# Linear-attention gates in four steps per head, and the decayed context keys formed inside the levels

## The chip, the cores and the metric

The kernel runs on one NeuronCore of one Trainium2 chip. The metric is device microseconds of one execution; lower is better. Engines are named as in the profile: PE (TensorE matmuls), PEld (its weight loads), DVE (VectorE), ACT (ScalarE), POOL (GpSimd), SP (SyncE, which issues most loads).

## The reference, cut to what matters

The reference is one layer of a hybrid backbone for 256 latent tokens with a prefix of 256 context tokens and a width of 2048. One input projection feeds a windowed attention with 16 heads and a gated linear attention (GLA) with 4 heads, key width 256 and value width 512; both are merged, and a convolutional feed-forward block follows. The change lies in the GLA part, which runs in both directions:

```python
gf = log_sigmoid(lrf @ w_gate_f + b_gate_f) / 16      # and gb, its own weights
# context, need_out False: only end states
b = jnp.cumsum(g, axis=1)
w = jnp.exp(b[:, -1:] - b)
sf = einsum("bthd,bthe->bhde", k_ctx * w, v_ctx)       # sb: the same on the flipped tokens
# latent tokens, chunk by chunk, from S = sf (or sb)
o_inter = (q * exp(b)) @ S
A[t, s] = sum_d q[t, d] k[s, d] exp(b[t, d] - b[s, d])  # s <= t
o = o_inter + A @ v
```

All arithmetic is in 32-bit floats, and the depth is 1, so the context gives nothing but keys, values and end states.

## The kernel before, in words

Every large projection splits its float32 weights into a high part (`whi`, made on ACT, L207) and a low part (`wlo`, made on DVE, L208), and PE multiplies by both. `proj_nat` and `proj_T` walk over the 2048 input rows in eight pairs of 128. For each pair they load and split a 128 x 1024 weight piece (`wsplit`), run the matmuls with the high part and then those with the low part. In `proj_nat` over latent and context tokens (four token tiles) that is 16 matmuls with 512 columns, then 8.

Small work is woven into these projections. Python generators and lists hold steps, and there are two hooks per weight pair: `tick` ahead of the split, and `midway` between the high and the low matmuls. Both call `aside`, which adds a rate to a counter and resumes the generator in `beside` each time the counter passes one. The PE instructions that a step emits are pinned behind the last matmul of the projection emitted so far (`mm_b`, `turn_b`), so they can't run earlier than their hook. The instructions of other engines have no such pin. From all of this a planner lays down the order on each engine ahead of the run: it takes instructions by readiness as it estimates it, and by their order in the program. `in_order` adds a tie that orders two instructions of one engine and costs no semaphore. A tile gets one of a fixed number of buffers of its tag and waits until one is free.

The four GLA heads run one after the other through `with_gla`, beside one projection each: head 0 beside the key projection (`kb_block`), heads 1 to 3 beside the value projection of their own head (`v_block`; the last with `by_tile`, whose last pair goes tile by tile). A block has 16 hooks. `gla_A` yields between these steps:

- *Gates.* For each direction `d` and half `dt` of the key width: one matmul into `pz`, then on ACT an absolute value (L708), a relu (L710), an exponential and a logarithm (L711, L712). DVE adds the latent half into `segs` (L713), POOL the context half into `gc` (L714). Two halves make a step, so the gates take two steps.
- *Level 0 to 7.* The latent 256 x 256 matrix `A` is built from segments of doubling length m = 1, 2, ..., 128. A level makes `q2` and, from level 1 on, `k2` (two exponentials on ACT each, L753, L754, L760, L761, and a multiplication on DVE each, L755, L762), then updates the segment sums in place with two to four DVE additions (L764 to L767), of which L767 is the last. Then it issues the `products` of the level before: eight small matmuls into `pa` and a masked copy into `at` (L738). Level 1 yields once more ahead of its products.
- *Context.* After the products of level 7, `q2` and `q3` for the context (L780, L781) and the decayed context keys: four prefix scans over `gc` into `kf` and `kg` (L787, L789), the total `tot` (L791), three exponentials (L793, L794) and two multiplications with the context keys (L795, L796). Two yields later come the matmuls of `kf` and `kg` with `q2` and `q3`, and the split of the result into `atc`.

`gla_o` multiplies `ats` and `atc` with the values into `po`. Between the levels DVE also serves a background list, `mod_latent`: products of modulation rows with a sum (L365), in turns set by `bg_rate`. Behind head 3 POOL loads the rotary table into `rope`, which takes a buffer of the tag "fc" (six buffers, shared with `gc`, `ats`, `atc`), and multiplies it with the norms (L884, L886). `q2`, `k2`, `kf`, `kg` share the four buffers of tag "fa"; the gate temporaries `ge`, `gm`, the `junk` of `gla_o` and `norms` share the four of "fb".

Of the kernel before, what the change touches and what calls it, by code (L numbers as in the profile page):

```python
# [8 lines left out]
F32 = mybir.dt.float32  # L9
F32R = mybir.dt.float32r  # L10
U8 = mybir.dt.uint8
AF = mybir.ActivationFunctionType
ALU = mybir.AluOpType
# [3 lines left out]
P = 128  # L17
D = 2048
T = 256
# [12 lines left out]
def layer_kernel(ctx, tc, A, out):  # L32
    nc = tc.nc
    V, S, G, PE = nc.vector, nc.scalar, nc.gpsimd, nc.tensor
# [7 lines left out]
    sm = pool(name="sm", bufs=4)  # L42
# [7 lines left out]
    def M(name, shape, dt=F32):  # L50
        return big.tile(shape, dt, name=name, tag="M")

    def W2(tag, name, shape, dt=F32):
        return f2.tile(shape, dt, name=name, tag=tag, bufs=F2_BUFS[tag])
# [9 lines left out]
    def in_order(*ins):  # L64

        for a, b in zip(ins, ins[1:]):
            tc.add_manual_dep(b, a.name, mybir.DependencyInfo(
                mybir.DependencyClass.NoSync, mybir.DependencyReason.DATA), reason="order")
# [25 lines left out]
    def mm_b(*a, **k):  # L94
        return pe_seq(after(PE.matmul(*a, **k)))  # L95
# [33 lines left out]
    ones = cst.tile([P, P], F32, name="ones")  # L129
# [16 lines left out]
    beside = []  # L146
# [343 lines left out]
    def affine_shift(s, t0, n):  # L490
        for kt in range(t0, t0 + n):
            xk = xr[2 * s + kt // 8][:, kt % 8, :]
            sh = shift1[:, s, kt:kt + 1]
            hi, lo = hh[s][kt // 8][:, kt % 8, :], hl[s][kt // 8][:, kt % 8, :]
            j = S.activation(hi, xk, AF.Identity, bias=sh).ins
            i = V.scalar_tensor_tensor(lo, xk, sh, hi.bitcast(F32), op0=ALU.add, op1=ALU.subtract).ins
        return i, j
# [49 lines left out]
    i, j = affine_shift(0, *groups[0])  # L547
# [31 lines left out]
    i, j = affine_shift(1, *groups[1])  # L579
# [94 lines left out]
    for d in range(2):  # L674
        mk = sel[:, 32 + d:33 + d]
        S.activation(lr[:, d, :], pl, AF.Identity, scale=mk)
        for q in (32, 96):
            r = lr[q:q + 32, d, :]
            V.scalar_tensor_tensor(r, pl[q:q + 32, :], mk[q:q + 32, :], r.bitcast(F32),
                                   op0=ALU.mult, op1=ALU.subtract)  # L680
# [11 lines left out]
    def gla_A(h, kb, qb, res):  # L692
        k_ = kb[:, (h % 2) * 2:(h % 2) * 2 + 2, 0:T]
        kc = kb[:, (h % 2) * 2:(h % 2) * 2 + 2, T:2 * T]
        q_ = qb[:, 2 * h:2 * h + 2, :]
        R = M("segs", [P, 4, 2, T])
        PF, SB, SX, PX = (R[:, i] for i in range(4))
        G.memset(R[:, 2:4], 0.0)
        gc = []
        for d in range(2):  # L700
            g_ = W2("fc", "gc", [P, 2, T])
            for dt in range(2):
                f = 2 * h + dt
                pz = bank("pz", side=True)
                mm_b(pz, wg[:, f * P:(f + 1) * P], lr[:, d, :], start=True, stop=True)
                b = nbg[:, d * 8 + f:d * 8 + f + 1]
                e = W2("fb", "ge", [P, 512])
                S.activation(e, pz, AF.Abs, scale=-1.0, bias=b)  # L708
                mn = W2("fb", "gm", [P, 512])
                S.activation(mn, pz, AF.Relu, scale=-1.0, bias=b)  # L710
                S.activation(e, e, AF.Exp, scale=-1.0)  # L711
                S.activation(e, e, AF.Ln, bias=ones[:, 0:1])  # L712
                V.tensor_tensor((PF if d == 0 else SB)[:, dt, :], mn[:, 0:T], e[:, 0:T], op=ALU.add)  # L713
                G.tensor_tensor(g_[:, dt, :], mn[:, T:2 * T], e[:, T:2 * T], op=ALU.add)  # L714
            gc.append(g_)
            yield

        at = sm.tile([P, 2, P], F32, name="at", tag="at", bufs=1)
        pa = bank("pa", (P, 2, P), side=True)
        for t in range(2):  # L720
            for dt in range(2):
                mm_b(pa[:, t, :], k_[:, dt, t * P:(t + 1) * P], q_[:, dt, t * P:(t + 1) * P],
                          start=(dt == 0), stop=(dt == 1))
        V.tensor_scalar(at, pa, 2.0, None, op0=ALU.mult)

        def halves(x, m):
            v = x.rearrange("p d (n two h) -> p (d n) two h", two=2, h=m)
            return v[:, :, 0, :], v[:, :, 1, :]

        def products(lv, q2, k2):  # L730
            pa = bank("pa", (P, 2, P), side=True)
            for t in range(2):
                tq = t if lv < 7 else 1 - t
                for dt in range(2):
                    mm_b(pa[:, t, :], k2[:, dt, t * P:(t + 1) * P],
                              q2[:, dt, tq * P:(tq + 1) * P], start=(dt == 0), stop=(dt == 1))
            if lv < 7:
                V.copy_predicated(at, lmask[:, lv:lv + 1, :].to_broadcast([P, 2, P]), pa)  # L738
            else:
                split(ats[0][:, 0], ats[0][:, 1], at)  # L740
                split(ats[1][:, 0], ats[1][:, 1], pa)

        ats = [W2("fc", "ats", [P, 2, 2, P], F32R) for _ in range(2)]
        for lv in range(8):
            m = 1 << lv
            n = T // m
            pfL, pfR = halves(PF, m)
            sbL, sbR = halves(SB, m)
            sxL, sxR = halves(SX, m)
            pxL, pxR = halves(PX, m)  # L750
            q2 = W2("fa", "q2", [P, 2, T])
            qL, qR = halves(q2, m)
            S.activation(qR, pfR, AF.Exp, scale=-1.0 / 16)  # L753
            S.activation(qL, sbL, AF.Exp, scale=-1.0 / 16)  # L754
            V.tensor_tensor(q2, q2, q_, op=ALU.mult)  # L755
            k2 = k_
            if lv:
                k2 = W2("fa", "k2", [P, 2, T])
                kL, kR = halves(k2, m)
                S.activation(kL, sxL, AF.Exp, scale=-1.0 / 16)  # L760
                S.activation(kR, pxR, AF.Exp, scale=-1.0 / 16)  # L761
                V.tensor_tensor(k2, k2, k_, op=ALU.mult)  # L762
            if lv < 7:
                V.tensor_tensor(sxL, sxL, pfR[:, :, m - 1:m].to_broadcast([P, n, m]), op=ALU.add)  # L764
                V.tensor_tensor(pxR, pxR, sbL[:, :, 0:1].to_broadcast([P, n, m]), op=ALU.add)
            V.tensor_tensor(pfR, pfR, pfL[:, :, m - 1:m].to_broadcast([P, n, m]), op=ALU.add)
            V.tensor_tensor(sbL, sbL, sbR[:, :, 0:1].to_broadcast([P, n, m]), op=ALU.add)  # L767
            if lv == 1:
                yield
            if lv:  # L770
                products(lv - 1, *prev)
            prev = q2, k2
            yield
        products(7, *prev)


        q2 = W2("fa", "q2", [P, 2, T])
        q3 = W2("fa", "q3", [P, 2, T])
        for dst, e in ((q2, PF), (q3, SB)):
            S.activation(dst, e, AF.Exp, scale=-1.0 / 16)  # L780
            V.tensor_tensor(dst, dst, q_, op=ALU.mult)  # L781
        kf = W2("fa", "kf", [P, 2, T])
        kg = W2("fa", "kg", [P, 2, T])
        tot = sm.tile([P, 2], F32, name="tot", tag="tot", bufs=2)
        one = ones[:, 0:1].to_broadcast([P, T])
        for dt in range(2):
            V.tensor_tensor_scan(kf[:, dt, :], one, gc[0][:, dt, :], 0.0, op0=ALU.mult, op1=ALU.add)  # L787
            V.memset(kg[:, dt, 0:1], 0.0)
            V.tensor_tensor_scan(kg[:, dt, 1:T], ones[:, 0:1].to_broadcast([P, T - 1]), gc[1][:, dt, 0:T - 1], 0.0,  # L789
                                 op0=ALU.mult, op1=ALU.add)  # L790
        V.tensor_scalar(tot, kf[:, :, T - 1], -1.0 / 16, None, op0=ALU.mult)  # L791
        for dt in range(2):
            S.activation(kf[:, dt, :], kf[:, dt, :], AF.Exp, scale=1.0 / 16, bias=tot[:, dt:dt + 1])  # L793
        S.activation(kg, kg, AF.Exp, scale=-1.0 / 16)  # L794
        V.tensor_tensor(kf, kf, kc, op=ALU.mult)  # L795
        V.tensor_tensor(kg, kg, kc, op=ALU.mult)  # L796
        yield
        yield
        pa = bank("pa", (P, 2, T), side=True)
        for t in range(2):  # L800
            for i, (kk, qq) in enumerate(((kf, q2), (kg, q3))):
                for dt in range(2):
                    mm_b(pa[:, t, :], kk[:, dt, t * P:(t + 1) * P], qq[:, dt, :],
                              start=(i == 0 and dt == 0), stop=(i == 1 and dt == 1))
        atc = [W2("fc", "atc", [P, 2, T], F32R) for _ in range(2)]
        split(atc[0], atc[1], pa)
        res.extend((ats, atc))
# [32 lines left out]
    qbt = M("qb", [P, 8, T])  # L840
# [2 lines left out]

    def with_gla(h, kb, block):
        res = []
        beside[:] = [gla_A(h, kb, qbt, res), 0.91, 0.0]
        v = block()
        for _ in beside[0]:
            pass
        beside.clear()  # L850
        return res, v
# [322 lines left out]
    for half, blocks in enumerate((range(0, 6), range(6, 11))):  # L1174
        n = len(blocks)
# [128 lines left out]
```

## Time and profile before

| | |
|---|---|
| median of 3 runs | 1984.97 us (1984.95 to 1985.31) |
| profiled execution | 1985.05 us |
| its span, first to last instruction | 1983.1 us |
| PE busy | 1958.6 us (99%) |
| DVE busy | 1400.0 us (71%) |
| ACT busy | 971.2 us (49%) |
| granted TensorE clock | 0.999 |
| first gate matmul of heads 0 to 3 | 213.6, 278.7, 343.2, 407.2 us |

Times in rows count from the first instruction. A row of a timeline has the start, the length, the engine, the line, the operation, what it writes and reads, and, in brackets, how long the engine stood idle before it and who ended that. A row of waits has the total, the count and the longest. Lengths of consecutive instructions of an engine overlap a little.

### The profile page before, as it was taken

To read this page: it belongs to the slowest core of one execution; us is meant where nothing else is said; L and a number is where in the kernel's file an instruction comes from. 1 tells how busy PE (TensorE), PEld (TensorE's weight loads), DVE (VectorE), ACT (ScalarE), POOL (GpSimd) and SP (SyncE) were. 2 spreads that over 40 slices of the span, in tenths; PEclk is the share of its full clock that TensorE was granted. 3 is DMA by queue.
4 is the path that set the end of the run, shared out by engine and by line. 5 is a ranking of instruction groups with operands and counts; after the bars stand their busy time and mean duration, and the time that the engine had idled before them with its cause. 6 is when DMAs were issued, how large, how long until landed. Compare 5 with 4: busy or idle time off the path is not lost.

```text
span 1983.1 us, 27131 instructions
## 1 busy us (share of the span) xinstructions
PE 1958.6 (99%) x10324; PEld 1637.9 (83%) x10324; DVE 1400.0 (71%) x2150; ACT 971.2 (49%) x1413; POOL 44.5 (2%) x61
## 2 busy tenths in 40 slices
PE   7999999999999999999999999999999999999999
PEld 5679888888887788888888888888888888888887
DVE  5765667876858888777776457889887555677754
ACT  4323555553345666444444445755555334555532
POOL 0010010112000000000000000000000000000000
PEclk9999999999999999999999999999999999999999
DMA  9965222336753456888888668688886566666563
GB/s 379 413 262 178 65 85 75 107 98 196 249 156 112 127 181 210 267 289 287 295 281 272 232 224 282 193 271 278 259 275 232 192 193 190 190 190 184 190 215 113
DMA packets 183603, 420.90 MB, mean 212 GB/s; under 512 B 12544, under 2 KB 12768, under 8 KB 178736
## 3 DMA queue, kind: packets, MB, share of 16 engines
q1 hardware_dynamic: 181856, 413.19, 63.8%
q0 software_dynamic: 1440, 5.80, 1.0%
q8 instruction: 81, 1.33, 0.3%
q14 instruction: 50, 0.41, 0.1%
q10 hardware_dynamic: 176, 0.17, 0.0%
HBM read 416.98 MB, written 2.13 MB: 211 GB/s over the span
## 4 chain that ended last, share of the span: by engine, by line
PE 68%; DVE 0%; ACT 0%; issue 0%; DVEq 0%
PE acc L83 52%; PE accs L83 12%; PE poa L95 1%; PE pS L95 1%; PE ptp L98 1%; PE pto L98 0%; PE ptx L98 0%; DVE wlo L208 0%; ACT s L973 0%; PE ptq L98 0%; DVE s L978 0%; DVE yd L1225 0%; DVE yd L1219 0%; DVE raw L365 0%; ACT whi L207 0%
## 5 line engine op out<-in xcount | busy, mean ns | idle before, releaser
L208 DVE TENSOR_TENSOR wlo<-raw,whi 128x1024 fp32r<-128x1024 f32 x568 | 694.8, 1225 | 435.0 <-ACT whi L207 394.7
L207 ACT ACTIVATE whi<-raw 128x1024 fp32r<-128x1024 f32 x568 | 601.1, 1059 | 773.3 <-PE acc L83 619.4
L83 PE MATMUL accs<-h,whi 128*128 128x512 f32 x704 | 176.3, 392 | 0.0
L83 PE MATMUL acc<-h,whi 128*128 128x512 f32 x640 | 160.4, 392 | 0.0
L83 PEld LDWEIGHTS accs<-h,whi 128*128 128x128 f32 x704 | 126.6, 189 | 22.6
L83 PE MATMUL acc<-whi,h01hi 128*128 128x512 f32 x352 | 139.9, 398 | 0.0
L83 PE MATMUL acc<-whi,h00hi 128*128 128x512 f32 x352 | 139.0, 395 | 0.0
L83 PE MATMUL acc<-whi,h00lo 128*128 128x512 f32 x352 | 138.0, 392 | 0.0
L83 PE MATMUL acc<-whi,h01lo 128*128 128x512 f32 x352 | 137.9, 392 | 0.0
L83 PE MATMUL acc<-whi,al 128*128 128x512 f32 x352 | 137.0, 389 | 0.0
L83 PE MATMUL acc<-whi,ah 128*128 128x512 f32 x352 | 137.0, 389 | 0.0
L83 PEld LDWEIGHTS acc<-h,whi 128*128 128x128 f32 x640 | 115.1, 189 | 20.6
L83 PEld LDWEIGHTS accs<-h,wlo 128*128 128x128 f32 x704 | 96.0, 190 | 6.8
L83 PE MATMUL acc<-wlo,h01hi 128*128 128x512 f32 x352 | 98.7, 396 | 0.0
L83 PE MATMUL accs<-h,wlo 128*128 128x256 f32 x704 | 98.2, 282 | 0.0
L83 PE MATMUL acc<-wlo,h00hi 128*128 128x512 f32 x352 | 97.7, 394 | 0.0
L83 PE MATMUL acc<-wlo,ah 128*128 128x512 f32 x352 | 94.3, 389 | 0.0
L83 PEld LDWEIGHTS acc<-h,wlo 128*128 128x128 f32 x640 | 87.4, 190 | 6.3
L83 PE MATMUL acc<-h,wlo 128*128 128x256 f32 x640 | 89.4, 282 | 0.0
L365 DVE CUSTOM_DVE_ANT_0 raw<-raw,csrow,pack 128x1024 f32<-128x1024 f32 x64 | 81.7, 1284 | 0.0
L83 PEld LDWEIGHTS acc<-whi,ah 128*128 128x128 f32 x352 | 66.1, 188 | 13.7
L83 PEld LDWEIGHTS acc<-whi,al 128*128 128x128 f32 x352 | 66.1, 188 | 13.6
(389 smaller groups left out, 3566.0 us busy)
## 6 DMA issues: line engine op xcount, KB each, us to landing
raw<-in_w_in SPq DMA_DIRECT2D x208, 512.0 KB, 4.4
raw<-in_w_up SPq DMA_DIRECT2D x176, 512.0 KB, 3.9
raw<-in_w_modT SPq DMA_DIRECT2D x128, 512.0 KB, 4.6
raw<-in_w_down SPq DMA_DIRECT2D x88, 512.0 KB, 3.7
mraw<-in_w_mod SPq DMA_DIRECT2D x32, 1024.0 KB, 13.3
raw<-in_w_attn_o SPq DMA_DIRECT2D x32, 512.0 KB, 4.9
raw<-in_w_gla_o SPq DMA_DIRECT2D x32, 512.0 KB, 4.7
raw<-in_w_out SPq DMA_DIRECT2D x32, 512.0 KB, 4.8
```

Of the source, the lines that this page charges most:

```text
L83: r = pe_seq(PE.matmul(*a, **k))
L95: return pe_seq(after(PE.matmul(*a, **k)))
L98: return pe_seq(after(PE.transpose(*a)))
L207: j = S.activation(hi[:, 0:n, :], raw[:, 0:n, :], AF.Copy).ins
L208: i = V.tensor_tensor(lo[:, 0:n, :], raw[:, 0:n, :], hi[:, 0:n, :].bitcast(F32), op=ALU.subtract).ins
L365: i0 = V.tensor_tensor_reduce(out=raws[i], in0=raws[i], in1=row[0], scale=1.0, scalar=d if h else bmod[:, b0:b0 + 1], op0=ALU.mult, op1=AL ...
```

## The change

- Each gate piece is a step of its own: four steps in place of two. The extra yield in level 1 is gone.
- `kf` and `kg` are taken ahead of the levels, from the buffers "fb" instead of "fa". The scans of the first half follow level 2, those of the second half level 3, the total and the exponentials level 4, the multiplications level 6. Each of their DVE instructions is tied by `in_order` behind the last segment update of its level (and behind one another).
- The rate of `beside` goes from 0.91 to 0.97.

The instructions themselves stay the same in kind, number and size.

```diff
                 G.tensor_tensor(g_[:, dt, :], mn[:, T:2 * T], e[:, T:2 * T], op=ALU.add)
+                yield
             gc.append(g_)
-            yield
+
+        kf = W2("fb", "kf", [P, 2, T])
+        kg = W2("fb", "kg", [P, 2, T])
+
+        def decays(dt, level):
+            one = ones[:, 0:1].to_broadcast([P, T])
+            i = V.tensor_tensor_scan(kf[:, dt, :], one, gc[0][:, dt, :], 0.0, op0=ALU.mult, op1=ALU.add).ins
+            V.memset(kg[:, dt, 0:1], 0.0)
+            j = V.tensor_tensor_scan(kg[:, dt, 1:T], ones[:, 0:1].to_broadcast([P, T - 1]), gc[1][:, dt, 0:T - 1],
+                                     0.0, op0=ALU.mult, op1=ALU.add).ins
+            in_order(level, i, j)
+
+        def decayed(level):
+            tot = sm.tile([P, 2], F32, name="tot", tag="tot", bufs=2)
+            in_order(level, V.tensor_scalar(tot, kf[:, :, T - 1], -1.0 / 16, None, op0=ALU.mult).ins)
+            for dt in range(2):
+                S.activation(kf[:, dt, :], kf[:, dt, :], AF.Exp, scale=1.0 / 16, bias=tot[:, dt:dt + 1])
+            S.activation(kg, kg, AF.Exp, scale=-1.0 / 16)
+
+        def decayed_keys(level):
+            in_order(level, V.tensor_tensor(kf, kf, kc, op=ALU.mult).ins)
+            in_order(level, V.tensor_tensor(kg, kg, kc, op=ALU.mult).ins)
+
+        beside_levels = {2: lambda i: decays(0, i), 3: lambda i: decays(1, i), 4: decayed, 6: decayed_keys}
...
-            V.tensor_tensor(sbL, sbL, sbR[:, :, 0:1].to_broadcast([P, n, m]), op=ALU.add)
-            if lv == 1:
-                yield
+            level = V.tensor_tensor(sbL, sbL, sbR[:, :, 0:1].to_broadcast([P, n, m]), op=ALU.add).ins
             if lv:
                 products(lv - 1, *prev)
             prev = q2, k2
+            if lv in beside_levels:
+                beside_levels[lv](level)
             yield
...
-        kf = W2("fa", "kf", [P, 2, T])
-        kg = W2("fa", "kg", [P, 2, T])
-        tot = sm.tile([P, 2], F32, name="tot", tag="tot", bufs=2)
...
-        beside[:] = [gla_A(h, kb, qbt, res), 0.91, 0.0]
+        beside[:] = [gla_A(h, kb, qbt, res), 0.97, 0.0]
```

More of the change, by code (lines that the diff above doesn't have):

```diff
@@ L781, in gla_A @@
             V.tensor_tensor(dst, dst, q_, op=ALU.mult)
-        kf = W2("fa", "kf", [P, 2, T])
-        kg = W2("fa", "kg", [P, 2, T])
-        tot = sm.tile([P, 2], F32, name="tot", tag="tot", bufs=2)
[L785 to L796, printed above, removed]
         yield
```

## The prediction

> **What bounds the kernel now.** I read the page first.
>
> ```profile
> span 1983.1 us, 27131 instructions
> PE 1958.6 (99%) x10324; PEld 1637.9 (83%) x10324; DVE 1400.0 (71%) x2150; ACT 971.2 (49%) x1413; POOL 44.5 (2%) x61
> ```
>
> PE sets the end, and the change takes no matmul away. It can therefore win only time in which PE stands still inside the linear-attention (GLA) part, and lose only by new standstills. The profiled execution took 1985.05 us, 1.95 more than its span and 0.08 more than the median of the three runs. 0.2% of that is 4.0 us, about what a measurement of this kernel can tell from no change. Next I asked the view of waits for 213 to 480 us, where the four heads lie.
>
> ```profile
> PE pa L95 <- DVE q L755: 3.3, 4, 1.1
> PE pa L95 <- DVE kf L795: 2.5, 3, 1.0
> DVE kf L787 <- PE pa L95: 3.4, 2, 2.5
> ACT kg L794 <- DVE kg L789: 5.0, 2, 2.5
> POOL rope L876 <- DVE kg L788: 33.8, 1, 33.8
> ```
>
> PE waits once per head for the `q2` of level 0 (3.3 us together) and in three heads for the decayed context keys (2.5 us). Both are in the change's reach. An idle row is measured from the modelled end of a matmul, and matmuls overlap, so I looked at both places in head 1 in the timeline (start, length, engine, ...).
>
> ```profile
> 289.72 0.39 PE L83 MATMUL acc<-whi,h10hi 128*128 128x512 f32 x1
> 289.95 0.39 PE L83 MATMUL acc<-whi,h10lo 128*128 128x512 f32 x1
> 291.54 1.07 PE L83 MATMUL acc<-wlo,h00hi 128*128 128x512 f32 x4
> 293.68 1.16 PE L95 MATMUL pa<-q,kb 128*128 128x128 f32 x8 [1.08 <-DVE q L755]
> 307.75 0.62 PE L83 MATMUL acc<-wlo,h01hi 128*128 128x512 f32 x2
> 308.23 1.13 PE L95 MATMUL pa<-q,k 128*128 128x128 f32 x8
> 309.11 0.71 PE L83 MATMUL acc<-wlo,h01hi 128*128 128x512 f32 x2
> 310.80 0.39 PE L83 MATMUL acc<-whi,h01lo 128*128 128x512 f32 x1
> 311.17 1.02 PE L95 MATMUL pa<-q,k 128*128 128x128 f32 x7
> 321.69 1.05 PE L95 MATMUL pa<-q,k 128*128 128x128 f32 x8
> 328.74 0.67 PE L95 MATMUL pa<-q,kf 128*128 128x256 f32 x2 [0.54 <-DVE kf L795]
> ```
>
> Starts lie 0.23 apart (289.72, 289.95). Four from 291.54 would free PE at 292.46; it starts at 293.68, a hole of 1.22 where the row says 1.08. So a hole is 0.14 longer than its idle, and seven holes come to 3.3 + 2.5 + 7 x 0.14 = **6.8 us**. That is all there is to win.
>
> Then who is behind these waits: busy time in four stretches, each from the last gate to the decayed keys of a head (length; PE, PEld, DVE, ACT, POOL).
>
> ```profile
> 226.80:263.80 37.00, 36.00 (x305) 35.79 (x304) 32.82 (x69) 17.41 (x39) 0.00 (x0) 1.00 0.23 71
> 292.40:328.60 36.20, 34.72 (x181) 28.46 (x180) 34.31 (x71) 18.41 (x42) 0.95 (x1) 1.00 0.32 91
> 355.60:392.60 37.00, 35.79 (x188) 29.85 (x186) 35.61 (x72) 18.93 (x41) 1.53 (x2) 1.00 0.32 96
> 419.50:459.00 39.50, 37.72 (x195) 31.27 (x195) 39.05 (x78) 19.82 (x45) 2.81 (x5) 1.00 0.47 140
> ```
>
> DVE is free for 4.2, 1.9, 1.4 and 0.5 us. In heads 1 to 3 the levels and the context chain are one DVE queue, nearly without a gap: moving work inside it shortens nothing on DVE; it changes which product finds its operand late.
>
> **The change, part by part.** Rows of head 1, one of POOL and then DVE's:
>
> ```profile
> 290.59 1.48 POOL L714 TENSOR_TENSOR gc<-gm,ge 128x256 f32<-128x256 f32 x1 [0.60 <-ACT ge L712]
> ```
>
> ```profile
> 285.29 0.42 DVE L713 TENSOR_TENSOR segs<-gm,ge 128x256 f32<-128x256 f32 x1 [1.96 <-ACT ge L712]
> 289.31 0.97 DVE L713 TENSOR_TENSOR segs<-gm,ge 128x256 f32<-128x256 f32 x1
> 290.20 1.27 DVE L365 CUSTOM_DVE_ANT_0 raw<-raw,csrow,pack 128x1024 f32<-128x1024 f32 x1
> 291.40 0.95 DVE L713 TENSOR_TENSOR segs<-gm,ge 128x256 f32<-128x256 f32 x1
> 292.95 0.68 DVE L755 TENSOR_TENSOR q<-q,qb 128x512 f32<-128x512 f32 x1
> 307.39 0.68 DVE L762 TENSOR_TENSOR k<-k,kb 128x512 f32<-128x512 f32 x1
> 319.49 0.68 DVE L755 TENSOR_TENSOR q<-q,qb 128x512 f32<-128x512 f32 x1
> 321.29 1.29 DVE L781 TENSOR_TENSOR q<-q,qb 128x512 f32<-128x512 f32 x2
> 322.85 0.69 DVE L787 TENSOR_TENSOR_SCAN kf<-ones,gc 128x256 f32<-128x256 f32 x1
> 323.47 0.68 DVE L789 TENSOR_TENSOR_SCAN kg<-ones,gc 128x255 f32<-128x255 f32 x1
> 326.70 0.16 DVE L791 TENSOR_SCALAR tot<-kf 128x2 f32<-128x2 f32 x1
> 327.90 0.69 DVE L795 TENSOR_TENSOR kf<-kf,kb 128x512 f32<-128x512 f32 x1 [0.45 <-ACT kf L793]
> ```
>
> *Hooks.* A weight pair has two hooks, one before its 16 hi matmuls and one before its 8 lo ones; 16 per block. At rate 0.91 hooks 2 to 11 and 13 to 16 each run one step, at 0.97 hooks 2 to 16. Gates go from hooks 2, 3 to 2 to 5; level 0 from 4 to 6; the products of level 0 ("p0") from 6 to 7; p1 to p5 each one hook later (p5 from 11 to 12, empty before); p6, p7 and the `kf` products stay at 13, 14 and 16. The step count rises from 14 to 15, the hooks that run one too, so nothing spills behind the block.
>
> *The p0 wait.* Up to p0 PE gets the same gate matmuls and the same `at` product, and one lo part more. Without its hole PE was at p0, four lo matmuls behind hook 6, at 292.46; hook 7 is four matmuls on, at 293.4. The operand was there at 292.95 + 0.68 = 293.63. The last two gate sums L713 took 0.97 and 0.95 instead of 0.42, the second inside POOL's sum `gc` (290.59 to 292.07). With pieces a hook apart I let only the last one be so slow at the end, which brings the operand to about 293.1. So p0 waits for nothing; at worst 0.2 per head is left. Gain 3.3 + 4 x 0.14 = 3.9.
>
> *The `kf` wait.* What leaves the end is four scans at 0.62 (322.85 to 323.47), `tot` 0.1 and two multiplications of 0.69 at most (327.90), about 0.65 in a full queue: 3.9 us per head. Then the `kf` products want only the two `q` of L781, whose end moves from 322.58 to 326.5 at most; PE is there at 328.74 - 1.22 - 0.68 = 326.8 (both holes taken out). No wait: gain 2.5 + 3 x 0.14 = 2.9. The scans' wait for a "fa" buffer (the 3.4 us row) goes too, as `kf`, `kg` sit in "fb", whose gate tiles are done by level 2; next late after it are the `q` of L781.
>
> *What is queued behind the moved work.* The ties put scans, `tot` and multiplications behind a level's last update on DVE, ahead of the next level's `q2`, `k2`; PE's p3 to p7 wait for those. p7: hook 14 without the hole is 321.69 - 1.22 = 320.5; its operand came at 319.49 + 0.68 = 320.17, and comes 3.9 later less what fills idle DVE time (about 1): 323.1, so 2.6 late. p4 takes p5's old hook: 311.17 less two matmuls 0.46, one product 0.88 (308.23 to 309.11) and 1.22 makes 308.6; its operand, 308.07 before, comes four scans later, 310.5: 1.9 late. Late against its hook is not yet a wait: the order on PE is laid down beforehand by a planner, and the rows show it pushing a product back (at 308.23 p4 stands behind two lo matmuls of a part of eight, its operand 0.16 ahead of it, no idle). It costs what the planner doesn't foresee. Bounds per head: 0, if it foresees all; 3.9, if PE stands for the whole insertion. I take one slow gate sum, 0.97 - 0.42 = 0.55, which is no longer paid at p0 and runs on down a full queue, in heads 1 to 3: 1.7. It lies nearest to p0, the one error of plan that the trace shows with its cause.
>
> *POOL and the other queues.* The rope load waits 33.8 us on POOL for head 3's scans to free a "fc" buffer. Now that happens at level 3. In head 1 level 4's operand came 308.07 - 292.40 = 15.7 behind the start of the stretch, so in head 3 the load goes out near 419.5 + 15.7 = 435 instead of 455.6, and its multiplications 4.4 later, beside the last levels instead of the block's end.
>
> ```profile
> L876 POOL DMA_DIRECT2D rope<-in_k_rope x1: 544/544/544, 455.6 to 455.6; - x1
> L886 POOL TENSOR_TENSOR att<-rope,norms x8: 317/1295/1312, 460.4 to 468.5; 128x64 f32<-128x64 f32 x8
> L884 POOL TENSOR_TENSOR att<-rope,norms x4: 451/458/1438, 460.0 to 467.8; 128x128 f32<-128x128 f32 x4
> 460.07 1.42 DVE L365 CUSTOM_DVE_ANT_0 raw<-raw,csrow,pack 128x1024 f32<-128x1024 f32 x1
> 461.42 1.33 DVE L365 CUSTOM_DVE_ANT_0 raw<-raw,csrow,pack 128x1024 f32<-128x1024 f32 x1
> ```
>
> Beside them DVE's L365 takes 1.33 to 1.42 instead of 1.27. I take the lower, 0.05 for each of 12: 0.6 on a DVE with no slack. Upper bound: DVE stands for each at its shortest, 4 x 0.451 + 8 x 0.317 = 4.3. The Trainium skill ("SBUF — State Buffer", "SBUF: two separate sides") says that a DVE operation with two SBUF inputs and a GpSimd operation that reads SBUF take a shared port pair as an exclusive lock, and the second one blocks fully. By it the term would be up to the 4.3. The trace agrees only in part, as L713 beside `gc` lost 0.55 and L365 beside rope 0.06 to 0.15.
>
> ACT gets its three decay exponentials at level 4 instead of the end; it is busy for half of the stretches, so nothing. SP's loads and their order stay.
>
> **Sum.** 6.8 - 1.7 - 0.6 = 4.5 us: 1985.05 - 4.5 = 1980.55, and 0.08 less for the median: **1980.4 us**.
>
> **The rivals.** *A, the waits come back in the levels.* For it: heads 2 and 3 have 1.4 and 0.5 us of idle DVE, so the late products stay late; the three `kf` holes have no cause in the rows, and if the scans themselves run longer than planned, their 2.9 moves with them to p4. Then 6.8 - 1.7 - 0.6 - 2.9 leaves 1.6: 1983.4. If DVE stands for all of POOL's operations, 4.3 instead of 0.6, 4.5 - 3.7 leaves 0.8: 1984.2; that is what the lock would do (Trainium skill, as above). That the planner places the decays late in spite of the ties, which only forbid earlier, leaves the `kf` wait, again 1.6: 1983.4. Against it: p1 to p5 have no waits, so the planner's times for levels are good. Chance 0.30, all within 0.2%.
>
> *B, slower.* PE stands at p4 to p7 for the whole inserted work: the planner believes the operands are there and leaves the products at their hooks, while DVE is behind by 3.9 in heads 1 to 3. 11.7 - 6.8 = +4.9: 1989.9. It decides from 6.8 us of waits for `q2`, `k2` on (10.8 for 0.2%). For it: a full DVE, p7 2.6 late. Against it: the product at 308.23, placed in time. Chance 0.25.
>
> **How the numbers follow.** The forecast, faster by over 0.2% (below 1981.0), has 0.45; its own range runs from 1977.5 (all 6.8 won, and 0.7 by gates that end sooner) to 1981. A has 0.30, B 0.25. The range 1977.5 to 1990.5 takes in B at its price and leaves out some 0.1 above and less below.
>
> **What would show it.** Right: no wait of PE for L755 at level 0 nor for `kf`; under 3 us of waits of PE for `q2`, `k2` in all; scans between the updates of levels 2 and 3 on DVE; rope on POOL near 435. Wrong: PE waiting for L755 or L762 at levels 3 to 7 by over 3 us (A) or 7 us (B), or for `wlo`.

## The result and the profile after

The changed kernel takes 1982.24 us (median of 22 runs, 1981.69 to 1984.05) against 1985.34 us for the kernel before, measured with it. The ratio is 0.9984, with a 95% interval from 0.9979 to 0.9990: 3.1 us faster, which is 0.16%. A second measurement gave 0.9986 (0.9977 to 0.9994). The forecast was 4.5 us, with a range that holds the result; but the result lies within the 0.2% that the prediction gave to rival A.

The page after the change, its span and its engines:

```profile
span 1979.9 us, 27108 instructions
PE 1955.3 (99%) x10324; PEld 1636.8 (83%) x10324; DVE 1398.4 (71%) x2150; ACT 970.8 (49%) x1413; POOL 42.4 (2%) x61
```

Each engine's counts are the ones of before; only 23 instructions that aren't counted as work are fewer. To see where the 3.2 us of span lie, here are the first gate matmul (`pz`, first start in the row) and the first matmul behind the projections of the four heads (`ptq`), from the rows of these two tiles: first of before, then of after.

```profile
L95 PE MATMUL pz<-wgl x16: 389/389/469, 213.6 to 409.7; 128*128 128x512 f32 x16
L98 PE MATMUL ptq<-pack,sq x32: 270/272/328, 590.0 to 713.4; 128*128 128x128 f32 x32
```

```profile
L95 PE MATMUL pz<-wgl x16: 389/389/403, 213.4 to 412.2; 128*128 128x512 f32 x16
L98 PE MATMUL ptq<-pack,sq x32: 270/272/328, 586.8 to 710.2; 128*128 128x128 f32 x32
```

The stretch between them went from 590.0 - 213.6 = 376.4 to 586.8 - 213.4 = 373.4. 3.0 us of the gain are in this stretch, which is called the stage below. What PE and POOL's rope load waited for in its part with the four heads (205 to 480 us):

```profile
PE pa L95 <- DVE k L786: 3.5, 5, 1.0
PE pa L95 <- DVE q L779: 0.5, 1, 0.5
POOL rope L885 <- DVE kg L724: 13.9, 1, 13.9
```

The wait for the decayed keys `kf` is gone, and of the four waits for the `q2` of level 0 only head 0's is left. But PE now waits five times for a `k2` of the levels (L786 is the former L762, L779 the former L755). With the prediction's 0.14 us for each wait, the holes are 4.0 + 6 x 0.14 = 4.8 us, where they were 6.8.

Two of the five are alike: the products of level 4 ("p4") in heads 1 and 2. In the timeline of head 1, first PE and then DVE:

```profile
304.43 1.05 PE L95 MATMUL pa<-q,k 128*128 128x128 f32 x8
305.23 1.17 PE L83 MATMUL acc<-wlo,h01hi 128*128 128x512 f32 x4
306.24 1.07 PE L83 MATMUL acc<-wlo,h11hi 128*128 128x512 f32 x4
308.31 1.13 PE L95 MATMUL pa<-q,k 128*128 128x128 f32 x8 [1.00 <-DVE k L786]
```

```profile
305.02 0.68 DVE L723 TENSOR_TENSOR_SCAN kf<-ones,gc 128x256 f32<-128x256 f32 x1
305.63 0.68 DVE L725 TENSOR_TENSOR_SCAN kg<-ones,gc 128x255 f32<-128x255 f32 x1
306.23 0.67 DVE L779 TENSOR_TENSOR q<-q,qb 128x512 f32<-128x512 f32 x1
...
307.48 0.68 DVE L786 TENSOR_TENSOR k<-k,kb 128x512 f32<-128x512 f32 x1
```

The second pair of scans runs from 305.02 to 306.23, right ahead of level 4's `q2` and `k2`. The last operand is there at 307.48 + 0.68 = 308.16, and PE, through with eight low matmuls at about 307.15, starts at 308.31. The other three waits for `k2` are in head 3. There the rope load, which waited 33.8 us for its buffer before and now waits 13.9, leaves in the middle of the levels, and POOL's multiplications run beside the later ones:

```profile
433.15 0.54 POOL L885 DMA_DIRECT2D rope<-in_k_rope  x1 [13.88 <-DVE kg L724]
436.18 1.26 POOL L893 TENSOR_TENSOR att<-rope,norms 128x128 f32<-128x128 f32 x1 [2.49 <-DVE wlo L208]
437.41 1.58 POOL L895 TENSOR_TENSOR att<-rope,norms 128x64 f32<-128x64 f32 x2
...
439.46 0.95 DVE L786 TENSOR_TENSOR k<-k,kb 128x512 f32<-128x512 f32 x1
```

### The profile page after: what moved, and what is told of

It is laid out like the page before. It is cut to its first block, busy times and chain, and to the rows that moved or that the text cites. A ratio compares the mean times of both kernels' runs of the same rounds, so it can differ in the third digit from the quotient of the medians.

```text
span 1979.9 us, 27108 instructions
## 1 busy us (share of the span) xinstructions
PE 1955.3 (99%) x10324; PEld 1636.8 (83%) x10324; DVE 1398.4 (71%) x2150; ACT 970.8 (49%) x1413; POOL 42.4 (2%) x61
## 4 chain that ended last, share of the span: by engine, by line
PE 94%; DVE 3%; DMA 1%; ACT 1%; issue 1%; SPq 0%; DVEq 0%; ACTq 0%
PE acc L83 73%; PE accs L83 12%; PE pa L95 2%; PE poa L95 1%; PE pm L95 1%; PE pS L95 1%; PE po L95 1%; PE ptp L98 1%; DMA mraw<-in_w_mod 1%; DVE wlo L208 1%; PE plr L665 0%; PE pto L98 0%; DVE q L779 0%; ACT whi L207 0%; DVE k L786 0%
## 5 line engine op out<-in xcount | busy, mean ns | idle before, releaser
L365 DVE CUSTOM_DVE_ANT_0 raw<-raw,csrow,pack 128x1024 f32<-128x1024 f32 x64 | 81.5, 1282 | 0.0
```

What stands on the lines that cost most here:

```text
L365: i0 = V.tensor_tensor_reduce(out=raws[i], in0=raws[i], in1=row[0], scale=1.0, scalar=d if h else bmod[:, b0:b0 + 1], op0=ALU.mult, op1=AL ...
```

## The experiments

Three causes of the standstills that came back were set against each other: the scans run longer than the planner counts (rival A's condition); the slow gate sum of the prediction runs on through a full DVE queue; POOL's rope work slows DVE in head 3. The table gives the median, the kernel before as measured with it, the ratio with its interval, PE's waits for `q2`, `k2` and `kf` (us, times), and the stage as defined above, from the profiled execution.

| kernel | us | before | ratio | waits | stage |
|---|---|---|---|---|---|
| before | | | | 5.8, 7 | 376.41 |
| after | 1982.24 | 1985.34 | 0.9984 (0.9979 to 0.9990) | 4.0, 6 | 373.37 |
| gates_only | 1980.95 | 1985.17 | 0.9977 (0.9968 to 0.9986) | 3.6, 5 | 372.21 |
| decays_only | 1986.42 | 1985.17 | 1.0007 (0.9998 to 1.0015) | 6.2, 12 | 377.45 |
| sums_for_scans | 1980.55 | 1985.17 | 0.9974 (0.9964 to 0.9984) | 1.7, 2 | 370.53 |
| rope_late | 1980.49 | 1985.17 | 0.9977 (0.9968 to 0.9986) | 3.0, 4 | 372.01 |
| sums_rope_late | 1977.71 | 1985.04 | 0.9961 (0.9948 to 0.9973) | 0.5, 1 | 369.01 |
| no_ties | 1986.26 | 1985.04 | 1.0002 (0.9993 to 1.0011) | 7.4, 5 | 376.26 |
| scans_in_gates | 1980.98 | 1985.04 | 0.9980 (0.9971 to 0.9988) | 3.1, 6 | 372.32 |
| scans_no_sum | 1978.12 | 1985.04 | 0.9962 (0.9949 to 0.9974) | 0.8, 3 | 369.35 |
| after_again | 1983.39 | 1985.41 | 0.9986 (0.9977 to 0.9994) | 4.0, 6 | 373.32 |
| gates_again | 1981.21 | 1985.41 | 0.9978 (0.9969 to 0.9987) | 3.7, 5 | 372.41 |
| scans_again | 1979.76 | 1985.41 | 0.9965 (0.9952 to 0.9979) | 0.8, 3 | 369.38 |

The stages repeat within 0.2 us; the medians scatter more, in part for a reason told at the end, and so differences of one or two us are read from the stages. Edits are shown against the changed kernel where nothing else is said; `...` stands for lines left out.

**One half of the change at a time.** `gates_only` has the four gate steps, the rate 0.97 and no yield in level 1, and leaves the decayed keys behind level 7, as before. Against the kernel before:

```diff
                 G.tensor_tensor(g_[:, dt, :], mn[:, T:2 * T], e[:, T:2 * T], op=ALU.add)
+                yield
             gc.append(g_)
-            yield
...
-            if lv == 1:
-                yield
...
-        beside[:] = [gla_A(h, kb, qbt, res), 0.91, 0.0]
+        beside[:] = [gla_A(h, kb, qbt, res), 0.97, 0.0]
```

> Only the gates go in four steps (with the yield of level 1 gone and the rate 0.97); the scans and the decayed keys stay behind level 7 as before. Theory 1 (the scans run longer than the planner reckons, wherever they stand): the waits for q2 at level 0 go in heads 1 to 3, the waits for kf stay at their 2.5 us, no wait at p3 to p6; 3.0 us faster than before, about 1982.3. Theory 2 (the slow gate sums beside POOL put DVE behind its plan, and where p0 no longer waits the delay runs on down the queue): the waits for kf grow by what p0 no longer pays, from 2.5 to about 4 us, or p1 to p5 wait; 1 us faster than before, about 1984.

PE's waits in it:

```profile
PE pa L95 <- DVE kf L793: 2.7, 3, 1.1
PE pa L95 <- DVE q L755: 0.5, 1, 0.5
PE pa L95 <- DVE k L762: 0.4, 1, 0.4
```

The gates by themselves take away level 0's wait in heads 1 to 3 and keep the wait for `kf`. What runs on from the gates into the levels is one new wait for a `k2` (0.4 us) and 0.2 us more at `kf`. So the slow gate sum explains little. The gates alone, 1.2 us shorter in the stage, do better than the whole change. They also do better than expected, by 4.2 us instead of 3.0; the section on the prediction comes back to this.

`decays_only` has the decays inside the levels and keeps two gate steps, the rate 0.91 and the yield:

```diff
-                yield
             gc.append(g_)
+            yield
...
+            if lv == 1:
+                yield
...
-        beside[:] = [gla_A(h, kb, qbt, res), 0.97, 0.0]
+        beside[:] = [gla_A(h, kb, qbt, res), 0.91, 0.0]
```

> Only the decays go into levels 2 to 6 (tied, in buffers fb); gates in two steps, rate 0.91, the yield of level 1 kept. Theory 1: waits for q2 at level 0 stay (3.3 us), the kf waits go, and products p3 to p5 wait about 1.0 us once in each of heads 1 to 3: within 1 us of the kernel before, 1984.5 to 1986. Theory 2: p0's wait puts PE back in step with DVE, so after it nothing waits: 2.5 to 2.9 us faster than before, about 1982.5.

```profile
PE pa L95 <- DVE k L786: 3.6, 8, 0.9
PE pa L95 <- DVE q L779: 2.6, 4, 1.1
```

The wait for `kf` is gone here too, and eight waits for `k2` stand in its place, where three were expected. 3.6 + 8 x 0.14 = 4.7 us came back for the 2.9 that were won. Moving the decays alone gains nothing (interval 0.9998 to 1.0015).

**The scans' length.** `sums_for_scans` takes the whole change and puts an addition over both halves in place of each scan:

```diff
-            one = ones[:, 0:1].to_broadcast([P, T])
-            i = V.tensor_tensor_scan(kf[:, dt, :], one, gc[0][:, dt, :], 0.0, op0=ALU.mult, op1=ALU.add).ins
+            i = V.tensor_tensor(kf, gc[0], gc[0], op=ALU.add).ins
...
-            j = V.tensor_tensor_scan(kg[:, dt, 1:T], ones[:, 0:1].to_broadcast([P, T - 1]), gc[1][:, dt, 0:T - 1],
-                                     0.0, op0=ALU.mult, op1=ALU.add).ins
+            j = V.tensor_tensor(kg, gc[1], gc[1], op=ALU.add).ins
```

> The changed kernel with each scan of 256 elements replaced by an addition of 512 elements on DVE (0.68 us like a scan), at the same place with the same ties; the context sums are left out, so the output is another one. Theory 1: the planner knows additions well, so the waits at p4 of heads 1 and 2 (1.0 us each) fall under 0.3 and head 3 loses about 1 us of its waits: 3 us faster than the changed kernel, about 1979.3. Theory 2: DVE has the same work and the gates are the same, so the waits stay: 1982.2.

One of these additions, and PE around p4 in head 1:

```profile
305.53 0.68 DVE L722 TENSOR_TENSOR kf<-gc 128x512 f32<-128x512 f32 x1
...
306.73 1.07 PE L83 MATMUL acc<-wlo,h11hi 128*128 128x512 f32 x4
307.64 0.39 PE L83 MATMUL acc<-whi,h01hi 128*128 128x512 f32 x1
307.68 0.68 DVE L784 TENSOR_TENSOR k<-k,kb 128x512 f32<-128x512 f32 x1
...
308.32 0.39 PE L83 MATMUL acc<-whi,h01lo 128*128 128x512 f32 x1
308.55 1.09 PE L95 MATMUL pa<-q,k 128*128 128x128 f32 x8
```

The addition lasts 0.68 us, exactly as long as the scan that it replaces, so DVE is no less busy. DVE's order shifts a little, but p4's last operand is there at 307.68 + 0.68 = 308.36, not earlier than the 308.16 of the changed kernel. Yet p4 does not wait: four matmuls of the next weight piece (307.64 to 308.32) now stand ahead of it in the fixed order. So it is not DVE's time that leaves the hole, but the order that goes with the scans. Why it differs is inferred: the planner seems to count too little for the scan and about the right length for the addition, and then it fills the time. The plan's own figures are in no trace, and the addition also reads and writes both halves, which a plan may treat in another way. The waits that are left:

```profile
PE pa L95 <- DVE k L784: 1.2, 1, 1.2
PE pa L95 <- DVE q L777: 0.5, 1, 0.5
```

The first is in head 3, beside the rope work. The median lies 1.2 above the expected 1979.3; the stage, 2.8 us shorter than in the changed kernel, is near the 3 us that were expected.

**The rope load.** `rope_late` holds the load back behind head 3's `atc`:

```diff
-    G.dma_start(rope, A["k_rope"])
+    late = G.tensor_tensor(gate, a[1][0][:, 0, 0:2].bitcast(F32), scale1[:, 0, 12:14], op=ALU.add)
+    with tc.issue_after(late.ins):
+        G.dma_start(rope, A["k_rope"])
```

> The changed kernel with the load of the rotary table held back on POOL until head 3's last context product is split, so that its 12 multiplications stand behind the levels again. If they cost DVE time in head 3 (theory 3): of head 3's three waits (0.68, 0.57 and 0.71 us as holes, 1.96 together) some 0.8 go, so that head 3 is like heads 1 and 2 with 1.16: 1981.4. If not: 1982.2, same waits.

Its wait for `k2`, and three DVE groups of head 3 (404 to 455 us; count, busy time and mean ns of one), first of `rope_late`, then of after:

```profile
PE pa L95 <- DVE k L786: 2.5, 3, 1.0
...
L786 DVE TENSOR_TENSOR k<-k,kb 128x512 f32<-128x512 f32 x7 | 4.8, 681 | 0.0
L365 DVE CUSTOM_DVE_ANT_0 raw<-raw,csrow,pack 128x1024 f32<-128x1024 f32 x3 | 3.8, 1272 | 0.0
L791 DVE TENSOR_TENSOR segs<-segs 128x256 f32<-128x256 f32 x8 | 3.3, 416 | 0.0
```

```profile
L786 DVE TENSOR_TENSOR k<-k,kb 128x512 f32<-128x512 f32 x7 | 5.0, 721 | 0.0
L365 DVE CUSTOM_DVE_ANT_0 raw<-raw,csrow,pack 128x1024 f32<-128x1024 f32 x3 | 4.1, 1362 | 0.0
L791 DVE TENSOR_TENSOR segs<-segs 128x256 f32<-128x256 f32 x8 | 3.5, 434 | 0.0
```

Two waits go, 3.5 - 2.5 + 2 x 0.14 = 1.3 us, where 0.8 was expected, and the stage is 1.4 shorter. Each of the three groups is longer beside the rope work: 7 x 40 + 3 x 90 + 8 x 18 = 694 ns. The `q2` multiplications (L779) lengthen too, 8 x 32 ns. So POOL's twelve multiplications cost DVE time, and in a full queue that time becomes PE's. The wait that stays in head 3 is p4's: it ends at 435.12 in the changed kernel, ahead of the first of these multiplications (436.18).

`sums_rope_late` joins both edits.

> Both edits together: additions of 512 elements in place of the scans (the context sums are left out, so the output is another one) and the rope load held back. If theories 1 and 3 hold side by side, the three waits of the changed kernel in heads 1 to 3 (1.16, 1.16 and 1.96 us as holes) all go and only head 0's 0.65 at level 0 is left: under 1 us of waits of PE in the four heads, 1982.2 - 1.7 - 1.3 = 1979.2. If the two overlap (the one wait of 1.31 in head 3 stays without rope beside it), 1980.5.

```profile
PE pa L95 <- DVE q L777: 0.5, 1, 0.5
```

No wait for a `k2` is left. The stage is 373.37 - 369.01 = 4.4 us shorter than after's; the two edits by themselves gave 2.84 and 1.36, together 4.2. Two causes, then, that add: the scans, 2.9 us of holes, and the rope work, 1.3. The time fell below the expected 1979.2, to 1977.71.

**The ties.** `no_ties` is the whole change without its `in_order` calls.

```diff
-            in_order(level, i, j)
...
-            in_order(level, V.tensor_scalar(tot, kf[:, :, T - 1], -1.0 / 16, None, op0=ALU.mult).ins)
+            V.tensor_scalar(tot, kf[:, :, T - 1], -1.0 / 16, None, op0=ALU.mult)
...
```

> The changed kernel without in_order: scans, total and multiplications of the decays may stand where the planner likes. If the ties hold the decays away from the updates of a level, the scans now come forward into level 0 or 1 (their inputs are ready there) and p1 or p2 wait: 1 to 3 us slower than the changed kernel, 1983 to 1985. If the planner puts them into the same gaps by itself: the same order and 1982.2.

```profile
PE pa L95 <- DVE q L778: 6.3, 4, 1.6
...
290.74 0.69 DVE L723 TENSOR_TENSOR_SCAN kf<-ones,gc 128x256 f32<-128x256 f32 x1
...
293.37 0.39 DVE L713 TENSOR_TENSOR segs<-gm,ge 128x256 f32<-128x256 f32 x1
293.69 0.68 DVE L725 TENSOR_TENSOR_SCAN kg<-ones,gc 128x255 f32<-128x255 f32 x1
...
294.61 0.68 DVE L778 TENSOR_TENSOR q<-q,qb 128x512 f32<-128x512 f32 x1
```

Untied, the scans start as soon as POOL has formed `gc`, ahead of level 0's `q2` (294.61), and every head waits there, 1.6 us at the longest. A fifth wait, 1.1 us for a `k2`, is also left. The stage is 2.9 us longer than in the changed kernel, and the gain of the gates is lost again (ratio 1.0002). The ties are needed.

**Another place for the scans.** If the levels are full, the scans may go where DVE has idle time, among the gates. `scans_in_gates` puts each scan behind POOL's sum, in its gate step, with `kf` and `kg` in "fc" and the rope load held back.

```diff
                 G.tensor_tensor(g_[:, dt, :], mn[:, T:2 * T], e[:, T:2 * T], op=ALU.add)
+                if d == 0:
+                    V.tensor_tensor_scan(kf[:, dt, :], ones[:, 0:1].to_broadcast([P, T]), g_[:, dt, :], 0.0,
+                                         op0=ALU.mult, op1=ALU.add)
...
```

> The scans move from levels 2 and 3 into the gate steps, each behind its POOL sum, where DVE has idle time; total, exponentials and key multiplications stay in levels 4 and 6; rope held back. Theory 1: the error of the scans' plan is spent before level 0, where p0 has room for 0.14 to 0.2 us only, so some of it shows at p0 (0.3 to 0.6 us a head) and the waits at p4 go: 1979.5. If POOL's sums hold up the last scan and with it level 0, p0 waits by 1 us or more in each head: 1982.

```profile
PE pa L95 <- DVE q L775: 2.5, 4, 0.9
...
284.21 0.69 DVE L717 TENSOR_TENSOR_SCAN kf<-ones,gc 128x256 f32<-128x256 f32 x1 [0.64 <-POOL gc L715]
...
291.36 0.95 DVE L714 TENSOR_TENSOR segs<-gm,ge 128x256 f32<-128x256 f32 x1
292.24 0.67 DVE L721 TENSOR_TENSOR_SCAN kg<-ones,gc 128x255 f32<-128x255 f32 x1
```

The levels are nearly free of waits, but now DVE stands behind POOL's sum (0.64 us), the last gate sum still takes 0.95, and level 0 is late again in all four heads. The time, 1980.98, lies between the two that were expected.

`scans_no_sum` removes the sum: the scan adds the two gate halves itself, and POOL's 16 sums fall away. `kf` and `kg` take the "fc" buffers of `gc`, and so the rope load leaves late again, at 452.94 us.

```diff
-                G.tensor_tensor(g_[:, dt, :], mn[:, T:2 * T], e[:, T:2 * T], op=ALU.add)
+                if d == 0:
+                    V.tensor_tensor_scan(kf[:, dt, :], mn[:, T:2 * T], e[:, T:2 * T], 0.0, op0=ALU.add, op1=ALU.add)
+                else:
+                    V.memset(kg[:, dt, 0:1], 0.0)
+                    V.tensor_tensor_scan(kg[:, dt, 1:T], mn[:, T:2 * T - 1], e[:, T:2 * T - 1], 0.0,
+                                         op0=ALU.add, op1=ALU.add)
...
-        beside_levels = {2: lambda i: decays(0, i), 3: lambda i: decays(1, i), 4: decayed, 6: decayed_keys}
+        beside_levels = {4: decayed, 6: decayed_keys}
```

> The scans stand in the gate steps and add both gate halves themselves (add, add), so the 16 POOL sums are gone, and rope's buffer comes free only at the end of head 3, as in the kernel before. Both the scans' and the POOL sums' part of DVE's delay leave the levels, and 2.4 us of DVE work per head with them: no wait of PE at p1 to p7 and none for kf, at most head 0's 0.65 at level 0: 1978.0 to 1979.0. If the delays in the levels had another cause than scans and POOL, waits of about 1 us stay in heads 1 to 3: 1981.

```profile
PE pa L95 <- DVE k L779: 0.6, 2, 0.3
PE pa L95 <- DVE q L772: 0.2, 1, 0.2
...
290.22 0.43 DVE L713 TENSOR_TENSOR segs<-gm,ge 128x256 f32<-128x256 f32 x1 [0.18 <-ACT ge L712]
290.56 0.68 DVE L718 TENSOR_TENSOR_SCAN kg<-gm,ge 128x255 f32<-128x255 f32 x1
```

The last gate sum is back at 0.43 us, the scan follows with no wait, and all of PE's waits in the stage come to 0.8 us. This is the fastest of the kernels that leave nothing out: 6.9 us less than before, 0.9962.

**All three on one chip.** The whole change, its gate half and `scans_no_sum` were run together once more.

> The changed kernel once more, unaltered, beside the two it is to be compared with on one chip. So far it stands at 1982.2 us against 1985.3 before (3.1 less), the gates alone at 4.2 less on another chip. Theory (the decays in the levels give back more than the wait for kf that they take away): about 3.1 less than before, and about 1.1 more than the gates alone. Rival (the gap between the two came of the chips): within 0.4 us of the gates alone.

> Gates in four steps, decayed keys behind level 7 as before, on the same chip as the whole change. Theory: 4.2 us less than before, 1.1 less than the whole change. Rival: equal to the whole change within 0.4 us.

> Gates in four steps; the scans add the two gate halves themselves inside the gate steps, GpSimd's 16 sums are gone. Measured once as 7.0 us less than before. Theory (the scans leave the levels, the rope load leaves the stretch of head 3, the slow gate sums beside GpSimd go): again 6.5 to 7.5 less, and 4 less than the whole change. Rival (a matter of that chip): no more than 4.2 less than before, as the gates alone.

The order held: 1983.39, 1981.21 and 1979.76 against 1985.41. The whole change gained 2.0 by the medians, where 3.1 were expected, and 3.1 by the stages. The gates alone beat the whole change by 0.9 us in the stage; the medians' intervals overlap. `scans_no_sum` lay at 5.7 by the medians and 7.0 by the stages, less than expected by the former.

## Why the prediction was right, and where not

- *The p0 wait, 3.9 expected.* It went in heads 1 to 3. In head 0, 0.5 + 0.14 = 0.6 stays, so it brought 3.3. The limit "at worst 0.2 per head" failed there; the gate part alone shows the same 0.5, so the decays have no share in it.
- *The `kf` wait, 2.9 expected.* Gone altogether, as worked out. `decays_only` shows that the move of the decays, not the gates, takes it away.
- *What comes back in the levels, 1.7 expected.* This term was mis-sized and had the wrong cause. By the waits that vanish with the additions it is 2.9 us of holes: `sums_rope_late` has no wait for `k2`, `rope_late` three with 2.5 + 3 x 0.14 = 2.9. Their cause was named, but under rival A: "if the scans themselves run longer than planned, their 2.9 moves with them to p4". That is what happened in place, at p4 of heads 1 to 3, and as a sum in size. By head it is not the same (`kf` had waited 0.5, 1.0 and 0.9 us, p4 now waits 1.0, 1.0 and 0.5), so the equal sum is in part luck; and that the plan has the scans too short is inferred, as said above. The slow gate sum, on which the forecast rested, leaves one wait of 0.4 in `gates_only` and 0.2 more at `kf`.
- *Rope, 0.6 expected.* `rope_late` gives 1.3, a second mis-sized term. I had counted only L365's extra; the `q2`, `k2` and segment updates lengthen too. The load left at 433.15 where I had 435. The Trainium skill's rule ("SBUF — State Buffer", "SBUF: two separate sides") would have put the loss at up to 4.3; the trace agrees that the two engines get in each other's way, and its 1.3 us show that DVE isn't shut out for the whole of each POOL operation.
- *"That is all there is to win", 6.8.* This failed in the other direction. The holes fell by 6.8 - 4.8 = 2.0, the stage by 3.0. Taking the holes (waits + 0.14 each) off the stages leaves 369.6 for before and for `decays_only`, and 367.9 to 368.6 for all kernels with four gate steps. So the gate half, its steps and its rate together, brings another 1.0 to 1.7 us that no wait row shows; steps, rate and the dropped yield were not timed apart. The start times of PE's instructions in the traces show where most of it lies. Steps from one start to the next that are 0.06 to 0.12 us above the median of their kind come to 5.5 us in the stage of before and 5.3 in `decays_only`, but to 4.1 to 4.5 in all kernels with four gate steps. Nearly all stand where PE goes over from one tile to another, and there are ten to fifteen fewer of them. What makes them fewer isn't shown.
- *Rival B* did not come: the longest wait is 1.0, not 3.9. In heads 1 and 2 the products behind the late p4 stand without waits, as in head 3 without the rope work beside it (`rope_late`); p5 of head 1 stands at 313.39 in the middle of a low part, pushed back by the planner, as I argued from one product before.

So the sum as it was: 6.8 - 0.6 - 2.9 - 1.3 = 2.0, and 1.0 that wasn't counted, 3.0 where I had 4.5. Three terms were 2.5 too favourable together, and 1.0 that no term held made up for a part: that the forecast came so near is in that much luck. The range, 13 us wide, took in both rivals, and so it says little that it holds the result. By the sign that I had set (over 3 us of waits for `q2`, `k2` at levels 3 to 7) the 3.5 us row is rival A's, and so is a gain within 0.2%. The likeliest case, over 0.2%, was the wrong one by that measure, while its time was 1.8 us off.

## What to carry to other kernels

Where a fixed order is planned ahead, an operation that the plan seems to count too short (here inferred from a swap for another of the same traced length) can cost PE a wait wherever the queue is full. Look for such operations first, and put them where the engine has idle time. Moving work off one wait is worth only what its new neighbours can bear: here the same four scans cost 2.9 us behind level 7 and 2.9 us in the levels, and among the gates, once they no longer stood behind POOL and the rope load was late, all waits that were left came to 0.8 + 3 x 0.14 = 1.2 us. Split a change of two parts before keeping both.

## What the runs showed of the hardware

A prefix scan over 256 elements takes 0.68 us on DVE (305.02), an addition over 256 takes 0.43 (290.22 in `scans_no_sum`), and an addition over 512 takes 0.68 (305.53 in `sums_for_scans`). The Trainium skill ("DVE: opcode table, instruction layouts, handler registers and perf-mode slots", "6. Datapath and trigger behaviour") says that the built-in scan runs at half throughput; the trace agrees, with 0.68 for half the elements.

The granted clock can dip early. The stretch from 30 to 50 us (length; PE, PEld, DVE, ACT and POOL busy with counts; granted clock; DMA), first of after, then of `gates_again`, here with two rows of its timeline, the first matmul behind a wait and the first one of the next projection:

```profile
30.00:50.00 20.00, 16.58 (x142) 12.30 (x141) 12.72 (x34) 10.78 (x20) 0.00 (x0) 1.00 1.03 412
```

```profile
30.00:50.00 20.00, 16.19 (x132) 12.19 (x131) 12.54 (x32) 9.67 (x16) 0.00 (x0) 0.91 1.03 412
...
32.46 0.39 PE L83 MATMUL acc<-h00hi,whi 128*128 128x256 f32 x1 [2.02 <-ACT qb L503]
36.93 0.40 PE L83 MATMUL acc<-whi,h00hi 128*128 128x512 f32 x1
```

In `gates_only`, the same kernel at 1.00, these two matmuls start at 31.96 and 34.93. From the one to the other it takes 2.97 us, and `gates_again` takes 4.47: 1.5 us are lost at the lower clock, and 0.5 were lost ahead of it. Together they are the 2.0 us by which the first gate matmul of `gates_again` came later, at 215.4 instead of 213.4. Behind it both run alike (stages 372.41 and 372.21). That is as large as the effects here, 160 us ahead of them, which is why they were read from the stage. One execution of each kernel was profiled, so it isn't shown that all scatter of the medians has this cause.
